# Layer 1's output projection: eight row tiles instead of five taken over six operand tiles inside the mixer

## The chip, the core and the metric

The kernel runs on one core of one Trainium2 chip. The metric is device time in microseconds (us) of one execution on that core, lower is better. The core's engines each run their own instruction stream in order and wait on one another by semaphores: PE is TensorE (matmuls; PEld is its weight load, which overlaps), DVE is VectorE, ACT is ScalarE, POOL is GpSimd, and SP issues most DMAs. In order listings, "x3" is three equal instructions in a row.

## The reference

A two-layer decoder trunk over 16 learned meta tokens and 1024 positions, width 1024. Layer 0 mixes by RWKV-7 and a pooling mixer, layer 1 by differential attention (8 heads). What the change touches is the end of layer 1's mixer:

```
h1 = rmsnorm(h, g0)
o  = differential_attention(h1)           # 8 heads of 128 -> 1024 values a position
y  = o @ w_out                            # "output projection": 1024 -> 1024
h  = h + rmsnorm(y, g1)
h  = h + rmsnorm(relu2(rmsnorm(h, g2) @ w1) @ w2, g3)   # MLP
```

Meta positions are dropped from the result. All is float32, with results close to float32's.

## The kernel before

Activations lie transposed: 128 features on the partitions, positions along the free dimension. A product in near-float32 is made of three matmuls in fp32r: each weight and each operand is split into a high part (a cast on ACT) and a low part (a subtraction on DVE, in the mixer on POOL), and high*high, low*high and high*low are accumulated. `wslices`/`mm3` write these in the mixer (L377, L378, L379), `mms` in what follows (L691).

**The output projection of layer 1** has 8 row tiles (128 output features each). Each sums over 8 operand tiles (one per attention head), for 4 quarters c0 to c3 of 256 positions. A full quarter of a row tile is 8 x 3 = 24 matmuls of 128x256. It is done in two stages:

- `early`, inside the mixer: for row tiles 0 to 4, the sum over operand tiles 0 to 5 (heads 0 to 5), 18 matmuls a quarter into the PSUM tile `pse`; ACT copies it to `pz` (L527) and stores it from its own DMA queue (L528) to `part`, a scratch tensor in DRAM. It is a generator that yields after each quarter. The list `fill` holds the operand loads of six heads, then the steps of `early`, with the load of operand tile 6 (`load(6)`) put nine places ahead of its end. During the last head, `fill[:30]` runs between the steps of attention, and the rest of it after. The weights of a row tile are loaded by SP (L360), cast by ACT (L361) and split by POOL (L362).
- `late`, after the mixer: for row tiles 0 to 4 the remaining operand tiles 6 and 7 (6 matmuls a quarter), which DVE adds (L721) onto `ac`, the tile into which `part` was loaded (L673). Row tiles 5 to 7 are taken over all 8 operand tiles here (24 matmuls a quarter), and ACT copies them to `ac` (L723). The weights of this stage are `LW[1]`: `wl` in two pieces (operand tiles 6 and 7 of row tiles 0 to 4, 640 columns each) and three pieces of `wo` (row tiles 5 to 7, 1024 columns). They are loaded by SP (L669), cast by ACT (L670) and split by DVE (L671).

`late` then works by halves of 512 positions (half 0 is c0 and c1, half 1 is c2 and c3). As the tiles of a half get complete, ACT squares them (L677, L682) and DVE sums the squares into `ss0` or `ss1` (L683). `scale` has PE sum `ss` over the partitions (L733); ACT and DVE make the inverse root (L741 to L743, L747, L748). `norms` scales the half and adds the residual on DVE (L768, L769, eight of each; the residual `hh` is loaded by L755), squares on ACT (L771) and sums by PE (L733). `base` makes the MLP's operands (ACT L809, DVE L810). `plain` is the first product of the MLP with two blocks of its first weights, loaded by L836 and split by L856 (ACT) and L857 (DVE); DVE L868 takes its result. After both halves the operands of a seven-product scheme are built (L885 to L895, L817 to L821), and the main loop of the MLP starts.

The order on each engine is not that of the text: `late` records its work in a `Flow` object, which orders it by estimated costs (`F.pe`, `F.act`, `F.dve`, `F.dma`); the mixer is ordered by a tile scheduler. SP issues its DMAs in order and waits at each for its buffer and its source.

Of the kernel before, what the change touches and what calls it, by code (L numbers as in the profile page):

```python
# [7 lines left out]
F32 = mybir.dt.float32  # L8
# [6 lines left out]
P = 128  # L15
T = 1040
# [44 lines left out]
PLAN = ((('prep', 0, 3), ('proj', (9, 5, 1), 1)), (('invert', 0, 1), ('prep', 1, 1), ('proj', (3, 6, 14, 2, 10), 1)), (('chain', 0, 1), ('invert', 1, 1), ('prep', 2, 1), ('proj', (15, 7, 11), 1), ('pool', (0, 1), 1)), (('invert', 2, 1), ('chain', 1, 1), ('prep', 3, 1), ('proj', (16, 17), 3), ('pool', (2, 3), 1), ('load', (0, 1), 2)), (('load', (2, 3, 4, 5), 18),), (('early', 8, 4), ('invert', 3, 3), ('chain', 2, 1)), (('early', 24, 1), ('chain', 3, 2)))  # L61


LW = ((768, 768, 1024, 1024), (640, 640, 1024, 1024, 1024))


AFTER = {"PE": (.25, 0.0), "ACT": (.17, .13), "DVE": (.11, .12), "POOL": (.08, .05), "SP": (.1, 0.0)}
# [254 lines left out]
class Trunk:  # L322
# [208 lines left out]
    def ahead(self, l):  # L531
# [4 lines left out]
        self.opb = [pool.tile([P, 4 * NH], F32R, name=self.nm("opb")) for _ in range((2, 3)[l])]  # L536
        n = self.lw_n = LW[l]
        at, self.lw_at = 0, []
# [15 lines left out]
    def late(self, l, xs, part, hin, hmid, hout, pre, rsb):  # L554

        nc, tc, A = self.nc, self.tc, self.A
# [2 lines left out]
        NS, SUB = ((2, 260), (1, 512))[l]  # L559
        NB = 8 // NS  # L560
        off = (0, NM)[l]
        ne = (6, 5)[l]
        chunks = QS[l]
        ends = (CH, QS[1])[l]
        stack = contextlib.ExitStack()
# [971 lines left out]
    def mixer0(self):  # L1537
# [10 lines left out]
        with tc.tile_pool(name="yp", bufs=4) as self.yp:  # L1548
# [41 lines left out]
            with tc.tile_pool(name="dps", bufs=2, space=PSUM, reuse_waits="tile") as self.dps, \  # L1590
# [31 lines left out]
                self.late_x = xs  # L1622
                self.lw_n = LW[0]
                for i in (0, 1):
# [12 lines left out]
    def mixer1(self, hn):  # L1637
        tc, nc, A, dr = self.tc, self.nc, self.A, self.dr
        self.o1d = dr.tile([8, P, 1024], F32, name="o1d")
        part = dr.tile([5 * P, T], F32, name="part1")  # L1640
        lam_init = 0.8 - 0.6 * math.exp(-0.3)
        with tc.tile_pool(name="dps", bufs=2, space=PSUM, reuse_waits="tile") as dps, \
             tc.tile_pool(name="sps", bufs=2, space=PSUM, reuse_waits="tile") as sps, \
             tc.tile_pool(name="tps", bufs=1, space=PSUM, reuse_waits="tile") as tps, \
             tc.tile_pool(name="aps", bufs=1, space=PSUM, reuse_waits="tile") as aps, \
             tc.tile_pool(name="ep", bufs=1, reuse_waits="tile") as ep:
            self.dps, self.sps, self.tps, self.aps, self.ep = dps, sps, tps, aps, ep
            self.tp = ep
            self.cs = ep.tile([P, 2, T], F32, name="cs")
            nc.sync.dma_start(self.cs, A["rope"])  # L1650
            lv = ep.tile([P, 4, C], F32, name="lv")
            nc.sync.dma_start(lv, A["lamv"])
            self.identb = ep.tile([P, P], mybir.dt.bfloat16, name="identb")
            nc.vector.tensor_copy(self.identb, self.con[:, K_ID:K_ID + P])
            self.maskb = ep.tile([P, P], mybir.dt.bfloat16, name="maskb")
            cau = ep.tile([P, 512], F32, tag="sb", name="cau", bufs=4)[:, :P]
            nc.sync.dma_start(cau, A["con"][:, K_CAU:K_CAU + P])
            nc.vector.tensor_copy(self.maskb, cau)
            nc.vector.tensor_tensor(lv[:, 0:2], lv[:, 0::2], lv[:, 1::2], op=ALU.mult)
            l2 = ep.tile([P, 2], F32, name="l2")  # L1660
            nc.vector.tensor_reduce(l2, lv[:, 0:2], axis=mybir.AxisListType.X, op=ALU.add)
            nc.scalar.activation(l2, l2, AF.Exp)
            self.nlam = ep.tile([P, 1], F32, name="nlam")
            nc.vector.scalar_tensor_tensor(self.nlam, l2[:, 1:2], -lam_init, l2[:, 0:1], op0=ALU.add, op1=ALU.subtract)
            self.sub = ep.tile([P, 1], F32, name="sub")
            nc.vector.tensor_scalar(self.sub, self.par[:, C_SUB:C_SUB + 1], (lam_init - 1.0) * 0.5 / P, None, op0=ALU.mult)
            self.pt, self.ov = {}, {}
            wide = [w.rearrange("p a b -> p (a b)") for w in self.WP]
            self.ring, self.turn = [(wide[0], wide[1]), (wide[2], ep.tile([P, 1024], F32R, name="wpx"))], 0
            self.given = [((wide[0], wide[1]),), (None,)]  # L1670
            self.quarters = QS[1]
            xs = [[] for _ in QS[1]]
            early = self.early(xs, A["wo_1"], part, 6, 5)
            load = lambda k: [0 for _ in self.loads(xs, self.o1d, (k,), NM, 2)]
            fill = [lambda k=k: load(k) for k in range(6)] + [lambda: next(early)] * (4 * 5)
            fill.insert(max(len(fill) - 9, 6), lambda: load(6))
            qkv, first = self.attn_in(0, hn)
            for i in [0, 5, 1, 6, 10, 11, 2, 7, 3, 4, 12, 8, 9, 13, 14, 15]:
                first[i]()
            for b in (0, 1):  # L1680
                self.pt[0, b] = self.attn_block(0, b, qkv)
            for h in range(8):
                nxt, side = self.attn_in(h + 1, hn) if h < 7 else (None, fill[:30])
                main = self.attn(h, qkv, nxt)
                at = (0, 6, 12, 12, 14, 15, 16, 24, 24, 24, 24, 24, 24, 24, 29, 29) if h < 7 else [0 + i * 2 for i in range(len(side))]
                i = 0
                for n, f in enumerate(main):
                    while i < len(side) and at[i] <= n:
                        side[i]()
                        i += 1  # L1690
                    f()
                for f in side[i:]:
                    f()
                qkv = nxt
            for f in fill[30:]:
                f()
            for c in range(4):
                xs[c].append(self.x7[c])
            self.late_x = xs
        return part  # L1700
# [384 lines left out]
```

## Time and profile before

| what | value |
|---|---|
| median of 3 runs | 2776.96 us (2776.26 to 2778.88) |
| the profiled execution's own time | 2771.01 us |
| its span in the trace | 2769.1 us |
| mean granted TensorE clock | 0.974 of full speed |
| PE busy | 94% of the span |
| DVE busy | 73% |
| ACT busy | 48% |

The profiled execution is 5.95 us shorter than the median of the runs; 1.9 us of its own time lie outside the span of the trace. Times in the rows below count from the start of the span. Layer 1's output projection lies at about 1939 to 2089 us, the norms and the first products of the MLP go on to about 2147 us, and the MLP's main loop follows to the end.

### The profile page before, as it was taken

Reading aid. Unit: us, or ns where it says so; the run is one execution under the profiler, and the core shown is the slowest. Engines: PE = TensorE matmul, PEld = TensorE weight load, DVE = VectorE, ACT = ScalarE, POOL = GpSimd, SP = SyncE. Lnnn points to the kernel's source line nnn. Section 1 sums busy time; section 2 is a strip of 40 time slices with the busy share of each in tenths; the row PEclk is TensorE's granted clock in tenths of the full one; section 3 lists DMA queues with packets and bytes.
Section 4 is the critical chain, followed back from the end, with each engine's and each line's share of the span. In section 5 each row is a group of like instructions: output and inputs, shape, how many; then the busy total and the mean of one; then the engine's idle time right before and its main releaser. Section 6 shows DMA issues by size and latency. Waiting matters only on the chain.

```text
span 2769.1 us, 44824 instructions
## 1 busy us (share of the span) xinstructions
PE 2614.2 (94%) x16950; PEld 2381.9 (86%) x16950; DVE 2032.5 (73%) x3742; ACT 1342.7 (48%) x2779; POOL 290.4 (10%) x410
## 2 busy tenths in 40 slices
PE   7999998899999999999968999999889999999997
PEld 6899897899899999999956899898787788778877
DVE  5356876534977777888786887888648778778888
ACT  5456776544633334343344556555636333443342
POOL 0111334220000000000012222222000000000000
PEclk9999998899999999999988999999999999999998
DMA  4456777554324345443332222222243243543443
GB/s 152 172 183 187 244 220 222 179 162 150 142 101 170 137 164 193 169 153 132 107 112 73 59 77 68 62 67 62 77 159 137 103 167 150 194 172 137 152 160 122
DMA packets 198575, 391.27 MB, mean 141 GB/s; under 512 B 59984, under 2 KB 122328, under 8 KB 185944
## 3 DMA queue, kind: packets, MB, share of 16 engines
q1 hardware_dynamic: 171176, 348.24, 37.8%
q10 hardware_dynamic: 27184, 40.18, 4.0%
q8 instruction: 133, 2.18, 0.3%
q14 instruction: 82, 0.67, 0.1%
HBM read 240.06 MB, written 131.38 MB: 134 GB/s over the span
## 4 chain that ended last, share of the span: by engine, by line
PE 64%; DVE 10%; ACT 4%; issue 2%; DMA 2%; POOL 0%; DVEq 0%; SPq 0%; ACTq 0%; POOLq 0%
PE bank L691 44%; PE psq L377 2%; PE psq L378 2%; PE psq L379 2%; PE ps L292 1%; PE s L1824 1%; PE tr L1870 1%; PE s L1826 1%; PE xs L292 1%; ACT p L1843 1%; DVE ac L1072 1%; DVE ac L1073 1%; DVE opb L818 1%; PE av L1896 1%; DVE ac L1001 1%
## 5 line engine op out<-in xcount | busy, mean ns | idle before, releaser
L691 PE MATMUL bank<-opa,wp 128*128 128x260 f32 (+1 forms) x3296 | 658.9, 320 | 8.6 <-DVE wp L782 5.3
L691 PEld LDWEIGHTS bank<-opa,wp 128*128 128x128 f32 x3296 | 518.0, 189 | 60.1 <-DVE wp L782 6.8
L691 PE MATMUL bank<-opb,wp 128*128 128x260 f32 (+1 forms) x1150 | 348.4, 324 | 1.8 <-DVE ac L1001 1.8
L292 PE MATMUL ps<-opa,whi 128*128 128x346 f32 (+2 forms) x1008 | 268.3, 328 | 4.7 <-DVE ys L292 4.0
L691 PE MATMUL bank<-opa,hh 128*128 128x260 f32 (+1 forms) x1112 | 241.1, 321 | 8.0 <-DVE hh L782 5.3
L691 PEld LDWEIGHTS bank<-opb,wp 128*128 128x128 f32 x1150 | 216.9, 189 | 21.0 <-ACT opa L1024 2.2
L1001 DVE TENSOR_TENSOR ac<-bank,ac 128x520 f32<-128x520 f32 (+1 forms) x256 | 171.6, 691 | 67.8 <-PE bank L691 66.5
L691 PE MATMUL bank<-opa,opb 128*128 128x260 f32 (+4 forms) x1168 | 206.1, 306 | 11.6 <-ACT opb L670 7.2
L691 PEld LDWEIGHTS bank<-opa,hh 128*128 128x128 f32 x1112 | 185.9, 191 | 24.4 <-DVE hh L782 5.8
L691 PEld LDWEIGHTS bank<-opa,opb 128*128 128x128 f32 x1168 | 168.2, 194 | 22.6 <-ACT opb L670 7.6
L292 PEld LDWEIGHTS ps<-opa,whi 128*128 128x128 f32 x1008 | 181.1, 192 | 6.5 <-DVE ys L292 4.8
L691 PE MATMUL bank<-opb,hh 128*128 128x260 f32 (+1 forms) x616 | 180.6, 327 | 0.0
L781 ACT CAST wp<-raw 128x512 fp32r<-128x512 f32 (+1 forms) x138 | 80.3, 584 | 184.6 <-PE bank L691 179.0
L292 PE MATMUL ps<-opa,wlo 128*128 128x346 f32 (+2 forms) x504 | 158.4, 314 | 0.0
L781 ACT CAST wp<-ss 128x512 fp32r<-128x512 f32 (+1 forms) x130 | 76.7, 590 | 164.5 <-PE bank L691 143.6
L1843 ACT ACTIVATE p<-s,m 128x272 f32<-128x272 f32 (+7 forms) x128 | 95.4, 750 | 85.4 <-DVE m L1839 83.6
L691 PE MATMUL bank<-opa,tt 128*128 128x260 f32 (+1 forms) x648 | 130.5, 318 | 0.2 <-DVE tt L782 0.2
L691 PEld LDWEIGHTS bank<-opb,hh 128*128 128x128 f32 x616 | 117.7, 191 | 9.9
L377 PE MATMUL psq<-opa,wp 128*128 128x346 f32 (+2 forms) x352 | 117.5, 334 | 4.4 <-DVE rp L462 2.6
L362 POOL TENSOR_TENSOR wpx<-raw,wp 128x1024 fp32r<-128x1024 f32 (+1 forms) x14 | 34.4, 2459 | 785.8 <-PE bank L691 742.8
L379 PE MATMUL psq<-opa,wp 128*128 128x346 f32 (+2 forms) x352 | 113.4, 322 | 0.0
L691 PE MATMUL bank<-opb,opb 128*128 128x256 f32 (+4 forms) x456 | 111.3, 308 | 0.5 <-DVE tt L747 0.5
(408 smaller groups left out, 6561.9 us busy)
## 6 DMA issues: line engine op xcount, KB each, us to landing
raw<-in_w_dram SPq DMA_DIRECT2D x64, 1024.0 KB
hid<-ac SPq DMA_DIRECT2D x14, 1820.0 KB
hid<-ac SPq DMA_DIRECT2D x14, 1792.0 KB
hh<-hid SPq DMA_DIRECT2D x23, 1040.0 KB
hh<-hid SPq DMA_DIRECT2D x23, 1024.0 KB
pk<-sg ACTq DMA_DIRECT2D x32, 704.0 KB
lt<-pk SPq DMA_DIRECT2D x32, 704.0 KB
raw<-in_w_qkv_dram SPq DMA_DIRECT2D x24, 512.0 KB
```

What stands on the lines that cost most here:

```text
L292: one = eng, cost, lambda: fn(*args, **kw), r, w
L362: (lo or nc.gpsimd).tensor_tensor(lw[:, :n], raw[:, :n], hi[:, :n].bitcast(F32), op=ALU.subtract)
L377: nc.tensor.matmul(ps, wh, xh, start=(first and i == 0), stop=False)
L378: nc.tensor.matmul(ps, wl, xh, start=False, stop=False)
L379: nc.tensor.matmul(ps, wh, xl, start=False, stop=(last and i == n - 1))
L691: nc.tensor.matmul(ps, use(x), use(y), start=start and i == j == 0, stop=i == len(ws) - 1 and j == 2, skip_group_check=not start)
L781: F.act(n, lambda: nc.scalar.copy(use(t[0][:, :n]), src), r=rd, w=[z[0]] + claim)
L818: F.dve(4 * NH, lambda: tt(lo, use(src), hi.bitcast(F32), op=ALU.subtract), r=rd + wh, w=wl)
L1001: F.dve(NH, lambda d=d, q=q: tt(sv(d), q, sv(d), op=ALU.add), r=nq + nd, w=nd, ps=True)
L1072: F.dve(W, lambda d=d, k=k: stt(d, d, self.gcol(l, 3, k), y, op0=ALU.mult, op1=ALU.mult), r=nd + [ny], w=nd)
L1073: F.dve(W, lambda d=d, k=k: tt(d, d, use(H3[k // 4][:, k % 4, :W]), op=ALU.add), r=nd + [("H", k // 4, k % 4)], w=nd)
L1843: nc.scalar.activation(p[:, :L0], S[c][:, :L0], AF.Exp, bias=m2[:, c:c + 1], scale=0.125, accum_out=m2[:, 2 + c:3 + c])
```

## The change

`ne`, the number of row tiles that are taken over six operand tiles inside the mixer, goes from 5 to 8. So `early` does all eight row tiles and `part` has eight; `late` has 6 matmuls per quarter of every row tile, all added by DVE onto what `part` holds. The late weights are then two pieces of 1024 columns, and no `wo` pieces. `fill` has twelve entries more, and `load(6)` stands at its place 29 instead of 17.

```
-LW = ((768, 768, 1024, 1024), (640, 640, 1024, 1024, 1024))
+LW = ((768, 768, 1024, 1024), (1024, 1024))
...
-        ne = (6, 5)[l]
+        ne = (6, 8)[l]
...
-        part = dr.tile([5 * P, T], F32, name="part1")
+        part = dr.tile([8 * P, T], F32, name="part1")
...
-            early = self.early(xs, A["wo_1"], part, 6, 5)
+            early = self.early(xs, A["wo_1"], part, 6, 8)
             load = lambda k: [0 for _ in self.loads(xs, self.o1d, (k,), NM, 2)]
-            fill = [lambda k=k: load(k) for k in range(6)] + [lambda: next(early)] * (4 * 5)
+            fill = [lambda k=k: load(k) for k in range(6)] + [lambda: next(early)] * (4 * 8)
             fill.insert(max(len(fill) - 9, 6), lambda: load(6))
```

What it does to SP's order where `late` begins, first before, then after. `raw` are the two staging buffers of weights (`raw0` the one that the mixer uses too), `ac0` and `ac1` the two halves, `h2` the residual, `w1` the MLP's first weights.

```order
L360 DMA raw0_743<-in_wo_1_dram 128x768
L669 DMA raw0_743<-in_wl_1_dram 128x640
L669 DMA raw_20234<-in_wo_1_dram 128x1024 x2
L673 DMA ac0_20243<-part1_13700 128x5x512
L669 DMA raw0_743<-in_wl_1_dram 128x640
L755 DMA hh2355_20241<-h2_68 128x4x512
L755 DMA hh2356_20242<-h2_68 128x4x512
L673 DMA ac1_20244<-part1_13700 128x5x512
L669 DMA raw0_743<-in_wo_1_dram 128x1024
L836 DMA raw_20234<-in_w1_1_dram 128x2048
```

```order
L360 DMA raw0_743<-in_wo_1_dram 128x768 x4
L673 DMA ac0_20516<-part1_13700 128x8x512
L669 DMA raw0_743<-in_wl_1_dram 128x1024 x2
L755 DMA hh2379_20514<-h2_68 128x4x512
L755 DMA hh2380_20515<-h2_68 128x4x512
L673 DMA ac1_20517<-part1_13700 128x8x512
L836 DMA raw_20507<-in_w1_1_dram 128x2048
L836 DMA raw0_743<-in_w1_1_dram 128x2048
```

Before, one `wl` piece and two `wo` pieces stand ahead of the first load from `part`; after, no late weights do, and both `wl` pieces stand behind it.

PE's order from the last matmul of `early`, first before, then after (the first rows of each; `bank` is a PSUM tile, `opa` an operand of the projection, `opb` a split weight):

```order
L379 MATMUL pse2344_20191<-opa7_77,wp1252_6332 128x256
L691 MATMUL bank5_20250<-opa0_70,opb2347_20223 128x256
L691 MATMUL bank5_20250<-opa0_70,opb2348_20224 128x256
L691 MATMUL bank5_20250<-opa0_70,opb2347_20223 128x256 x2
L691 MATMUL bank5_20250<-opa0_70,opb2348_20224 128x256
```

```order
L379 MATMUL pse2368_20464<-opa7_77,wp1254_6334 128x256
L691 MATMUL bank0_20518<-opa1_71,opb2370_20495 128x256 x3
L691 MATMUL bank0_20518<-opa1_71,opb2371_20496 128x256 x3
L691 MATMUL bank1_20519<-opa1_71,opb2370_20495 128x256 x3
L691 MATMUL bank1_20519<-opa1_71,opb2371_20496 128x256 x3
```

Before, `late` opens with a full tile over eight operand tiles from the `wo` weights; after, with tiles of six matmuls, each of which needs both `wl` pieces. After `early` PE has 216 matmuls less: the row sum of `ss0` stood behind 204 matmuls of half 0 and 48 of half 1, and stands behind 96 and 30 now.

DVE's order around the scaling of half 0, first before, then after (`ac1` is half 1, `opb` in L857 a weight of the MLP):

```order
L683 TENSOR_TENSOR ss0_20236<-ss0_20236,tt2352_20238 128x512
L747 SCALAR_TENSOR_TENSOR tt2353_20239<-bank0_20245,tt2353_20239 128x512
L748 SCALAR_TENSOR_TENSOR tt2354_20240<-tt2353_20239,tt2354_20240 128x512
L768 SCALAR_TENSOR_TENSOR ac0_20243<-ac0_20243,par_61,tt2354_20240 128x512 x2
L769 TENSOR_TENSOR ac0_20243<-ac0_20243,hh2355_20241 128x512 x2
```

```order
L857 TENSOR_TENSOR opb2373_20504<-raw_20507,opb2373_20504 128x512
L857 TENSOR_TENSOR opa7_77<-raw0_743,opa7_77 128x512
L721 TENSOR_TENSOR ac1_20517<-ac1_20517,bank3_20521 128x256
L857 TENSOR_TENSOR opb2372_20497<-raw0_743,opb2372_20497 128x512
L721 TENSOR_TENSOR ac1_20517<-ac1_20517,bank6_20524 128x256
L747 SCALAR_TENSOR_TENSOR tt2377_20512<-bank0_20518,tt2377_20512 128x512
L748 SCALAR_TENSOR_TENSOR tt2378_20513<-tt2377_20512,tt2378_20513 128x512
L721 TENSOR_TENSOR ac1_20517<-ac1_20517,bank4_20522 128x256
L768 SCALAR_TENSOR_TENSOR ac0_20516<-ac0_20516,par_61,tt2378_20513 128x512 x2
```

Eight of half 1's sixteen adds (L721) and three of the eight L857 now stand ahead of the first L768; before, all ten of half 1's adds and all eight L857 stood behind the eight L768 and L769. From L810 on, and in the MLP's main loop, the order of DVE, ACT, PE and SP is the same as before but for single places.

## Rows read from the trace of the kernel before

**Rows 1.** The page of the profile: the span, and busy time of each engine with its share and instructions.

```profile
span 2769.1 us, 44824 instructions
...
PE 2614.2 (94%) x16950; PEld 2381.9 (86%) x16950; DVE 2032.5 (73%) x3742; ACT 1342.7 (48%) x2779; POOL 290.4 (10%) x410
```

**Rows 2.** Busy time of the engines in stretches of the span, whole program. Columns: stretch, its length in us, then for each engine busy us (and instructions), the granted TensorE clock as a share of full speed, the DMA engines' busy share, and what they moved.

```profile
1950.00:1970.00 20.00, 14.12 (x72) 10.85 (x72) 15.72 (x33) 13.35 (x31) 0.19 (x1) 0.84 0.23 73
2015.60:2024.10 8.50, 8.50 (x74) 8.43 (x72) 0.70 (x2) 1.68 (x5) 0.00 (x0) 1.00 0.40 108
2024.10:2031.40 7.30, 0.70 (x3) 0.28 (x1) 2.07 (x3) 3.19 (x4) 0.00 (x0) 0.75 1.00 378
2031.40:2035.20 3.80, 3.77 (x20) 3.77 (x21) 1.11 (x1) 0.00 (x0) 0.00 (x0) 0.59 1.05 388
2035.20:2039.00 3.80, 3.80 (x35) 3.80 (x34) 0.83 (x1) 1.32 (x3) 0.00 (x0) 1.00 1.05 397
2031.40:2062.50 31.10, 31.07 (x252) 31.07 (x252) 12.03 (x20) 9.05 (x17) 0.00 (x0) 0.95 0.43 165
2105.00:2147.00 42.00, 37.54 (x146) 26.98 (x144) 40.35 (x53) 26.11 (x35) 0.00 (x0) 1.00 0.25 93
```

**Rows 3.** PE in order of time where `early` ends and `late` begins. Columns: start, us, engine, line, operation, out<-in, shape, count, and in brackets the idle time before with what ended it.

```profile
2023.95 0.27 PE L379 MATMUL pse<-opa,wp 128*128 128x256 f32 x1
2028.80 0.58 PE L691 MATMUL bank<-opa,opb 128*128 128x256 f32 x1 [4.57 <-ACT opb L670]
2031.43 31.23 PE L691 MATMUL bank<-opa,opb 128*128 128x256 f32 x251 [2.06 <-DVE opb L671]
2062.50 1.02 PE L733 MATMUL bank<-ss,con 128*128 128x512 f32 x2
```

**Rows 4.** The instructions of the tiles `pse` and `pz`: count, then duration in ns (least, median, most), first and last start.

```profile
L377 PE MATMUL pse<-opa,wp x120: 274/281/681, 1939.5 to 2023.7; 128*128 128x256 f32 x120
...
L527 ACT COPY pz<-pse x20: 353/373/385, 1971.7 to 2024.3; 128x256 f32<-128x256 f32 x20
```

**Rows 5.** Weights of `early` on POOL: the same columns.

```profile
L362 POOL TENSOR_TENSOR wp<-raw,wp x13: 1834/2392/2815, 1446.1 to 2004.8; 128x1024 fp32r<-128x1024 f32 x10, 128x768 fp32r<-128x768 f32 x3
```

**Rows 6.** SP's DMA queue in order of time: start and length of an issue.

```profile
2022.22 0.38 SPq L673 DMA_DIRECT2D ac<-part  x1
2022.65 0.52 SPq L669 DMA_DIRECT2D raw<-in_wl_dram  x1
2023.21 1.70 SPq L755 DMA_DIRECT2D hh<-h  x2
2030.04 0.36 SPq L673 DMA_DIRECT2D ac<-part  x1
2030.44 0.53 SPq L669 DMA_DIRECT2D raw<-in_wo_dram  x1
2032.54 17.59 SPq L836 DMA_DIRECT2D raw<-in_w_dram  x2
```

**Rows 7.** What SP's queue waited for between 2020 and 2045 us: in total, times, longest.

```profile
SPq L836 <- DMA raw<-in_wo_dram: 7.0, 1, 7.0
```

**Rows 8.** ACT and its DMA queue, then DVE, in order of time, at the stores of `early` and the weights of `late`.

```profile
2020.41 0.33 ACTq L528 DMA_DIRECT2D part<-pz  x1
...
2030.00 1.04 ACT L670 CAST opb<-raw 128x1024 fp32r<-128x1024 f32 x1 [1.26 <-DMA part<-pz]
...
2030.15 2.36 DVE L671 TENSOR_TENSOR opb<-raw,opb 128x1024 fp32r<-128x1024 f32 x2 [3.54 <-DMA part<-pz]
```

**Rows 9.** DVE in order of time at the scaling of half 0.

```profile
2065.61 0.69 DVE L747 SCALAR_TENSOR_TENSOR tt<-bank,tt 128x512 f32<-128x512 f32 x1 [3.99 <-ACT tt L743]
...
2067.06 1.42 DVE L768 SCALAR_TENSOR_TENSOR ac<-ac,par,tt 128x512 f32<-128x512 f32 x2
...
2075.98 1.29 DVE L769 TENSOR_TENSOR ac<-ac,hh 128x512 f32<-128x512 f32 x2
```

**Rows 10.** DVE's groups between 2024 and 2147 us: count, busy us, mean ns of one, idle before.

```profile
L683 DVE TENSOR_TENSOR ss<-ss,tt 128x512 f32<-128x512 f32 x14 | 9.7, 691 | 5.5 <-ACT tt L682 4.8
L721 DVE TENSOR_TENSOR ac<-ac,bank 128x256 f32<-128x256 f32 x20 | 8.1, 420 | 9.7 <-PE bank L691 9.7
L857 DVE TENSOR_TENSOR opb<-raw,opb 128x512 fp32r<-128x512 f32 x6 | 3.9, 687 | 0.0
```

**Rows 11.** DVE in order of time: its waits between the scaling of half 0 and the main loop, and the main loop's first instruction.

```profile
2088.80 0.42 DVE L721 TENSOR_TENSOR ac<-ac,bank 128x256 f32<-128x256 f32 x1 [1.05 <-PE bank L691]
...
2101.47 0.69 DVE L868 SCALAR_TENSOR_TENSOR ss<-bank,rsb 128x512 f32<-128x512 f32 x1 [2.27 <-PE bank L733]
...
2103.52 0.69 DVE L747 SCALAR_TENSOR_TENSOR tt<-bank,tt 128x512 f32<-128x512 f32 x1 [1.36 <-ACT tt L743]
...
2140.53 0.69 DVE L868 SCALAR_TENSOR_TENSOR ss<-bank,rsb 128x512 f32<-128x512 f32 x1 [0.95 <-PE bank L691]
...
2146.62 0.68 DVE L782 TENSOR_TENSOR hh<-raw,hh 128x512 fp32r<-128x512 f32 x1
```

**Rows 12.** PE in order of time: the first product of the MLP, and the main loop's wait.

```profile
2089.07 0.39 PE L691 MATMUL bank<-opb,opb 128*128 128x512 f32 x1
...
2147.35 0.79 PE L691 MATMUL bank<-opa,hh 128*128 128x512 f32 x1 [2.26 <-DVE hh L782]
```

## The prediction

> **What bounds the kernel now.** The page comes first: PE is busy 94% of the span, DVE 73% [rows 1]. So on the whole matmuls set the time, and a change that keeps their number, as this one does, can only give or take where PE waits. The change reaches from the end of the mixer to the start of the MLP's main loop, so that stretch is read next, by the busy time of its parts [rows 2]. PE is full while `early` runs, nearly idle from 2024.1 to 2031.4 us, full until 2062.5, and at the end, from 2105 to 2147, it is DVE that is full (40.35 us of 42.0) while PE has 4.5 us to spare. The orders of time say why. `late` opens with a gap of 7.4 us between the end of `early` (2023.95 + 0.12 = 2024.07) and 2031.43, but for one matmul of 24 at 2028.80 [rows 3]: it waits for weights, and in that gap the DMA engines are busy all the time [rows 2]. After that stretch the first scaling on DVE starts at 2067.06 [rows 9], and the MLP's main loop starts when DVE has made its operands: PE waits 2.26 us for DVE at 2147.35 [rows 12]. From 2067.06 to 2146.62, when DVE turns to the main loop, its waits of 0.9 us or more are the four of [rows 11], 5.6 us together. So once half 0 is summed, **DVE's chain bounds the stretch**, and the question is when that chain begins.
>
> **The change, part by part.**
>
> *Matmuls.* 216 of 128x256 (3 row tiles, 4 quarters, 18) leave `late` and join `early`. In `early` 72 take 8.50 us [rows 2], 0.118 each; in `late` 251 take 31.07 [rows 2, 3], 0.124 each with the cold start in it, and 35 in 3.80 (0.109) right after it. The same work at the same price: no gain by itself. `early` now ends at 2024.07 + 216 x 0.118 (25.5) = E = 2049.6.
>
> *Copies and weights of `early`.* ACT gets 12 copies of 0.37 us [rows 4] and loses 12 of the same length in `late`; both lie beside PE. The three more weights take about 1.84 us each on POOL (the least of [rows 5], the narrow shape), against 8.5 us of matmuls per row tile, and are made one row tile ahead: hidden. Without that cover each would cost its 1.84 on PE.
>
> *Late weights.* Before, a `wl` and two `wo` pieces were issued ahead of the load from `part`; PE could begin with row tiles 5 and 6. After, each late tile needs both `wl` pieces, and both stand behind the load of half 0 of `part` on SP. That load can be issued only when c1 of the last row tile is stored: at 2022.22, 1.85 us ahead of the end of `early` [rows 6], its store having been issued at 2020.41 [rows 8]. So the new issue time is E - 1.85. It carries 2.10 MB (1024 rows by 512 by 4 bytes), was 1.31; each `wl` piece is 0.52 MB. The late weights of before, the `wo` piece issued at 2030.44, landed at about 2039.9: of the two DMAs behind it the second waited 7.0 us for it, from 2032.9 on [rows 6, 7]. From 2022.22 to 2039.9 that queue moved 1.31 + 0.33 + 2.10 + 1.31 + 0.52 = 5.57 MB in 17.7 us. At 397 GB/s [rows 2] these are 14.0 us, and 3.7 more for latency and what is left of other transfers. By the same price the second `wl` piece lands (2.10 + 1.05) / 0.397 + 3.7 = 11.6 us after the issue, at E + 9.8. Then ACT casts it (1.04, [rows 8]) and DVE subtracts (2.36 for two, 1.18, same rows): PE is at full work at E + 12.1 with 0.1 for the handoff, in place of E + 7.4. **The gap grows by about 4.7 us**, to 2061.7. Bounds: 7.4 if the weights came as fast as before, some 14 if the rate in the gap is the 378 GB/s of its row and stores of `early` still hold the queue.
>
> On that gap the Trainium skill speaks, in "DMA: Bandwidth & Descriptors", section "Queues, rings and completion order": all DMAs that SP issues share one queue row, and on each DMA engine the descriptors of a ring are consumed in order. By it nothing overtakes the load from `part`, and the gap is the 12.1 us; were the two served side by side, the weights would be there when 2.1 MB have moved, and the gap 9.4. The 7.0 us wait for the `wo` piece [rows 7] agrees with the first.
>
> *Cold start.* After the gap of before the granted clock was 0.59 for 3.8 us, with 20 matmuls where the next 3.8 us had 35 [rows 2], a loss of 15 x 0.109 = 1.6 us. After a longer gap the same loss stands once more.
>
> *Up to half 0's row sum.* Before it stood behind 252 matmuls, at 2062.50 [rows 3]. Now it stands behind 96 of half 0 and 30 of half 1: 126 x 0.118 = 14.9, with 1.6 for the cold start 16.5: 2061.7 + 16.5 = 2078.2. DVE has in that time 16 adds of half 0 (0.42 each), 7 sums (0.69) [rows 10] and some 6 us of half 1's adds and MLP weights, 17.5 us at most: close to PE's, and so not counted but kept as a risk. The **scaling of half 0 starts 15.7 us later**, plus an add of 0.42 that stands ahead of L768: +16.1, at 2083.2.
>
> *From there.* DVE has 2.9 us less behind that point: three L857 (0.69) and two adds (0.42) were drawn ahead of it [rows 10]. Of its 5.6 us of waits [rows 11] the two of PE's plain work (1.05 and 0.95) go, since PE then has more time ahead; those of 2.27 and 1.36 follow half 1's row sum through ACT and stay, as that sum comes last on PE again. 16.1 - 2.9 - 2.0 = **+11.2 us** at the main loop, whose order is the old one and which adds nothing. Bounds: all 5.6 absorbed gives +7.6, nothing but the 2.0 waits gives +14.1.
>
> *The MLP's first weights* (L836, 2 x 1.05 MB) are now queued behind `part` half 0, `wl`, `hh` and `part` half 1: 9.44 MB after the issue, 23.8 + 3.7 us, at E + 25.6. On ACT six casts of them, on DVE three L857 stand ahead of half 0's root, which is due at E + 29. They are hidden by some 2 us.
>
> Sum, against the profiled execution's 2771.01: 2782.2. It lies 5.95 under the median, so for the median **2776.96 + 11.2 = 2788.2, said as 2788.0**.
>
> **The rivals.**
>
> *PE stays the bound.* If DVE's chain had more slack than its rows say, only the longer gap is paid: +4.7 us, 2781.7, within 0.2% (5.6 us, about what a measurement of this kernel tells from no change). For it: PE is busy 94% of the span. Against: from 2105 on DVE is 96% busy [rows 2] and PE waits for it. It decides if the first product of the MLP (2089.07 before, [rows 12]) doesn't wait at each of DVE's L810.
>
> *Nothing is absorbed.* The 16.1 us come through whole: 2793.1, and about 2 more if the MLP's weights land over 2 us late or the clock falls once more as PE waits through the scaling. For it: the row sums of half 0's norm now stand on PE with few tiles between them, so PE waits there, and may go cold as it did in the first gap (0.59, [rows 2]). Against: 2.9 us of DVE's work has demonstrably moved ahead in its order.
>
> *Faster: the added row tiles fill PE's idle time in the last head.* From 1950 to 1970 PE is busy for 14.12 us of 20 [rows 2]. If 10 us of the added matmuls ran there and in the like stretch before, E would fall by 10, and with PE as the bound the end by 10 - 4.7: 2771.7. It decides from 4.7 us of filled idle time with DVE not in the way, 16.1 with it. Against: in PE's order the added matmuls stand behind those of row tile 4, and the last head's stretch is the same as before.
>
> **How the numbers follow.** The forecast (+7.6 to +14.1) 0.65; nothing absorbed, with the clock or the late weights, 0.16; PE stays the bound 0.15; faster 0.04. The range holds the first two and half of the third: 2780.5 to 2795.0. The forecast's cases and "nothing absorbed" are slower by over 0.2%: 0.81; the same 0.15; faster 0.04.
>
> **What would show it.** The profile of after: the first L691 of `late` some 12 us after the last L379, with DMA at full share; the L733 of `ss0` near 2078 and the first L768 near 2083; the MLP's first product near 2097 with waits on L810; L782 on DVE at about 2158; the main loop as long as before. The prediction is wrong if `wl` lands ahead of `part`, if the first L768 comes before 2079, or if DVE shows waits over 8 us between it and L782.

## The result, and the profile after

| | before | after |
|---|---|---|
| median | 2776.61 us (6 runs) | 2786.92 us (6 runs) |
| profiled span | 2769.1 us | 2784.9 us |
| ratio of times | | 1.0036, 95% interval 1.0025 to 1.0048 |

The change makes the kernel 10 us slower (7 to 13 by the interval); 2788.0 was forecast, with a range of 2780.5 to 2795.0. The two profiled executions differ by more, 15.8 us, but not all of that belongs to the change: `early` starts at 1939.5 in the one and 1942.9 in the other, on the same code before it, and from the main loop's first L782 to the end it is 622.5 and 624.9 us, on the same code too. So the executions are compared by two stretches inside them: the length of `early`, and **D**, from the end of `early` to L782. PE where `early` ends, in order of time, after (the rows that answer to [rows 3]):

```profile
2052.94 0.28 PE L379 MATMUL pse<-opa,wp 128*128 128x256 f32 x1
2062.56 0.58 PE L691 MATMUL bank<-opa,opb 128*128 128x256 f32 x1 [9.34 <-ACT opb L670]
2063.82 1.01 PE L691 MATMUL bank<-opa,opb 128*128 128x256 f32 x3 [0.68 <-DVE opb L671]
2065.11 16.01 PE L691 MATMUL bank<-opa,opb 128*128 128x256 f32 x122 [0.28 <-DVE opb L671]
2080.97 1.02 PE L733 MATMUL bank<-ss,con 128*128 128x512 f32 x2
```

`early` ends at 2053.06: 110.1 us after its start, 84.6 before, so 25.6 longer. The gap to full work is 12.05 us, 7.36 before. The row sum of `ss0` comes 27.9 us after the end of `early`, 38.4 before. Then SP's DMA queue and ACT in the gap, after (as [rows 6, 8]):

```profile
2051.24 0.38 SPq L673 DMA_DIRECT2D ac<-part  x1
2051.71 1.87 SPq L669 DMA_DIRECT2D raw<-in_wl_dram  x2
...
2061.46 1.04 ACT L670 CAST opb<-raw 128x1024 fp32r<-128x1024 f32 x1 [7.83 <-DMA raw<-in_wl_dram]
2062.75 1.05 ACT L670 CAST opb<-raw 128x1024 fp32r<-128x1024 f32 x1 [0.24 <-DMA raw<-in_wl_dram]
```

Both casts are released by the landing of `wl`, which was issued right behind the load from `part`. The granted clock is low behind the gap as it was before ([rows 2]): 21 matmuls in the first stretch, 34 in the next.

```profile
2065.10:2068.90 3.80, 3.79 (x21) 3.79 (x22) 1.26 (x3) 0.00 (x0) 0.00 (x0) 0.63 1.05 386
2068.90:2072.70 3.80, 3.80 (x34) 3.80 (x34) 2.78 (x7) 1.32 (x3) 0.00 (x0) 1.00 1.07 396
```

And DVE, after (as [rows 9, 11]):

```profile
2085.74 1.41 DVE L768 SCALAR_TENSOR_TENSOR ac<-ac,par,tt 128x512 f32<-128x512 f32 x2
...
2115.89 0.69 DVE L868 SCALAR_TENSOR_TENSOR ss<-bank,rsb 128x512 f32<-128x512 f32 x1 [1.61 <-PE bank L733]
...
2117.94 0.69 DVE L747 SCALAR_TENSOR_TENSOR tt<-bank,tt 128x512 f32<-128x512 f32 x1 [1.36 <-ACT tt L743]
...
2160.01 0.69 DVE L782 TENSOR_TENSOR hh<-raw,hh 128x512 fp32r<-128x512 f32 x1
```

Half 0's scaling starts 32.7 us after the end of `early` (43.0 before); counted from the start of `early`, it is 15.3 us later. The two waits of about 1 us on PE's plain work ([rows 11]) are gone, the other two are there. D is 106.95 us, 122.55 before. 25.6 - 15.6 = **+10.0 us** at the main loop: this is the measured loss, and it lies in this stretch. The ratios below leave out two executions, of 3229.66 us (four row tiles) and 8873.02 us (three), that lie far above all others of their kernels.

### The profile page after: what moved, and what is told of

It is laid out like the page before. It is cut to its first block, busy times and chain, and to the rows that moved or that the text cites. A ratio compares the mean times of both kernels' runs of the same rounds, so it can differ in the third digit from the quotient of the medians.

```text
span 2784.9 us, 44875 instructions
## 1 busy us (share of the span) xinstructions
PE 2617.6 (94%) x16950; PEld 2381.0 (85%) x16950; DVE 2038.3 (73%) x3751; ACT 1342.6 (48%) x2779; POOL 296.6 (11%) x413
## 4 chain that ended last, share of the span: by engine, by line
PE 63%; DVE 10%; ACT 4%; issue 2%; DMA 2%; SPq 0%; POOL 0%; DVEq 0%; ACTq 0%; POOLq 0%
PE bank L691 43%; PE psq L377 2%; PE psq L378 2%; PE psq L379 2%; PE ps L292 1%; PE s L1824 1%; PE tr L1870 1%; PE s L1826 1%; PE xs L292 1%; ACT p L1843 1%; DVE ac L1072 1%; DMA hh<-hid 1%; PE pse L377 1%; PE pse L378 1%; DVE opb L818 1%
## 5 line engine op out<-in xcount | busy, mean ns | idle before, releaser
L691 PE MATMUL bank<-opa,opb 128*128 128x260 f32 (+4 forms) x952 | 179.6, 311 | 15.2 <-ACT opb L670 11.9
L691 PEld LDWEIGHTS bank<-opa,opb 128*128 128x128 f32 x952 | 142.5, 195 | 25.5 <-ACT opb L670 12.3
```

The source lines that it names most:

```text
L691: nc.tensor.matmul(ps, use(x), use(y), start=start and i == j == 0, stop=i == len(ws) - 1 and j == 2, skip_group_check=not start)
```

## The experiments

All runs are set beside the kernel before on the same chip. "Local" is (length of `early` - 84.6) + (D - 122.55), from the profile of each; where `early` is longer or shorter than its matmuls make it by a fall of the clock within the last head, the text says so. The last column is the ratio in us of the kernel before.

| row tiles | what (`pz` below) | gap | D | local | measured ratio (95%) | in us |
|---|---|---|---|---|---|---|
| 8 | the changed kernel | 12.05 | 106.95 | +10.0 | 1.0036 (1.0025 to 1.0048) | +10 |
| 8 | `wl` ahead of `part` | 6.2 | 103.99 | +10.3 | 1.0024 (1.0011 to 1.0036) | +7 |
| 8 | `hh` ahead of `wl` | 19.35 | 114.24 | +17.3 | 1.0051 (1.0037 to 1.0064) | +14 |
| 8 | `wl` ahead, own `pz` | 4.7 | 105.30 | +8.3 | 1.0023 (1.0010 to 1.0035) | +6 |
| 5 | before, own `pz` | 3.95 | 120.19 | -2.3 | 0.9986 (0.9972 to 1.0000) | -4 |
| 7 | | 9.95 | 111.94 | +9.8 | 1.0015 (1.0003 to 1.0027) | +4 |
| 6 | first | 8.6 | 122.99 | +12.3 | 1.0042 (1.0030 to 1.0054) | +12 |
| 6 | second | 8.4 | 122.97 | +9.4 | 1.0033 (1.0018 to 1.0048) | +9 |
| 6 | own `pz` | 3.3, later 0.6 | 117.01 | +3.1 | 1.0013 (1.0002 to 1.0023) | +4 |
| 4 | | 2.4 | 123.88 | -7.1 | 0.9977 (0.9964 to 0.9991) | -6 |
| 4 | own `pz` | 2.4 | 123.49 | -7.5 | 0.9972 (0.9958 to 0.9985) | -8 |
| 3 | own `pz` | 11.2 | 145.65 | +2.8 | 1.0004 (0.9993 to 1.0015) | +1 |

**The queue.** First, the `wl` pieces ahead of the load from `part`, with the order on PE, ACT and DVE untouched:

```
-  F.dma(lambda raw=raw, i=i: nc.sync.dma_start(raw, self.lw_src(l, i)), ...)
+  F.dma(lambda raw=raw, i=i: None if l and i < 2 else nc.sync.dma_start(raw, self.lw_src(l, i)), ...)
-  F.dma(lambda h=i: nc.sync.dma_start(m[h][:, :ne], self.rows(part, off + NH * h, NH)), ...)
+  F.dma(lambda h=i: part_load(h), ...)   # for l and h == 0: both wl loads, then this one
```

> The changed kernel with one thing different: SP issues both wl pieces ahead of the load of half 0 from part; the order on PE, ACT and DVE is that of the changed kernel. D is the time from the end of early (the last L379) to the main loop's first L782 on DVE: 122.5 us before, 107.0 after, where early ends 25.5 us later; so after stands at +9.9. Theory (the gap is made by the queue, and half 0's scaling starts DVE's chain, which nothing absorbs any more): the gap falls from 12.1 to about 6.0, since the cast of the second wl piece then waits for a store of early whose buffer it takes over, and D falls by the same 6 to 101; time about +4 over before, 2781. Rival A (DVE's chain is bound elsewhere, by the load of part or of the MLP's weights): the gap falls and D stays at 105 to 107, time +8 to +10. Rival B (the loss is the added copies, stores and bytes): gap and D stay, time +10.

The gap fell to 6.2 as expected, and half 0's scaling came 4.4 us sooner after the end of `early`; D fell by 3.0, not 6. The clock took back the rest, in two places: more of its low stretch lay behind the shorter gap, and it fell once more behind half 1's scaling. These are its stretches right behind the gap, then that one (columns as in [rows 2]):

```profile
2071.00:2075.00 4.00, 4.00 (x19) 4.00 (x20) 1.26 (x3) 0.00 (x0) 0.00 (x0) 0.50 1.05 392
2075.00:2079.00 4.00, 4.00 (x28) 4.00 (x28) 1.82 (x5) 1.27 (x2) 0.00 (x0) 0.74 1.05 387
...
2140.00:2145.00 5.00, 5.00 (x18) 3.62 (x18) 5.00 (x9) 4.12 (x5) 0.00 (x0) 0.81 0.12 43
```

19 and 28 matmuls in two stretches of 4 us; in the changed kernel one stretch of 3.8 us was slow, and the next had 34. The low stretch itself is as long as in the changed kernel, 10 us; it began sooner, and the gap ended sooner still (the rows are in the last section). And behind half 1's scaling, where the changed kernel shows 1.00, the clock was 0.81, and DVE waited 1.4 us more there. (In this execution `early` took 3.3 us more than in the changed kernel's, on the same order, at a clock of 0.5 within the last head; without that the local sum is +7.0.) So the place in SP's queue is worth some 3 of the 10 us by D; the two ratios' intervals overlap. Rival B falls, since gap and D both moved; between the theory's D of 101 and rival A's 105 to 107 the run does not decide.

The opposite dose, `hh` between `part` and `wl`:

```
-  F.dma(lambda raw=raw, i=i: nc.sync.dma_start(raw, self.lw_src(l, i)), ...)
+  F.dma(lambda raw=raw, i=i: wl_load(raw, i), ...)   # for l and i == 0: both hh loads, then this one
-  F.dma(lambda q=q: nc.sync.dma_start(H[q], ...), ...)
+  F.dma(lambda q=q: None if l and not h else nc.sync.dma_start(H[q], ...), ...)
```

> The changed kernel with the two loads of the residual hh (2.1 MB) issued between the load of half 0 from part and the wl pieces, so that these are 2.1 MB further back; all else in the same order. Theory: 2.1 MB at 0.397 MB a us are 5.3 us: gap 12.1 to 17.4, D 107.0 to 112.3, time about +15 over before. Rival A (slack of some us behind the gap): gap 17.4, D 108 to 110. Rival C (transfers of one queue are served side by side): the gap grows by under 3 us.

The gap grew to 19.35 and D to 114.24, 7.3 more in both: **behind the gap nothing absorbs any of it**. Rivals A and C fall. The size was off: 2.1 MB took 7.3 us and not 5.3. SP needed 4.3 us to issue the two `hh` loads, but that is not where the time went: the DMA engines were full all the while. These are the issues, a stretch of the gap (columns as in [rows 2]), the second cast, and what SP's queue moved from the issue of the load from `part` to that cast (packets, MB, share of the 16 engines), last the same for the changed kernel:

```profile
2049.95 4.30 SPq L678 DMA_DIRECT2D hh<-h  x2
2054.34 3.28 SPq L679 DMA_DIRECT2D raw<-in_wl_dram  x2
...
2053.00:2068.00 15.00, 0.00 (x0) 0.00 (x0) 0.00 (x0) 0.96 (x1) 0.00 (x0) 0.61 1.04 396
...
2068.34 1.04 ACT L670 CAST opb<-raw 128x1024 fp32r<-128x1024 f32 x1 [0.25 <-DMA raw<-in_wl_dram]
...
q1 hardware_dynamic: 2933, 6.37, 92.5%
...
q1 hardware_dynamic: 1520, 3.54, 84.7%
```

The loads up to the second `wl` piece are 5.24 MB here and 3.15 MB in the changed kernel. So 1.1 MB of loads that were issued behind it had moved by then, where it was 0.4 MB: 2.8 MB more at 0.396 MB a us are 7.1 us.

**The memory of `pz`.** In [rows 8] the casts and splits of the `wo` pieces, which SP had issued ahead of the load from `part`, are released by a store of `pz`: these late weights lie where `pz` lay. One line at the start of the mixer's pool gives `pz` a place of its own:

```
             self.cs = ep.tile([P, 2, T], F32, name="cs")
+            pz = [self.tmp("pz", 2) for _ in (0, 1)]
```

> The kernel before with the two pz buffers at a place of their own, all orders unchanged. In the kernel before the casts L670 at 2027.70 and the split L671 at 2030.15 are released by stores of pz. Theory (the gap of 7.4 us there was the stores of early, not the weights, which had been loaded): the casts follow one another after the last copy, gap 7.4 to about 4.5, D 122.5 to 119.5, time about 3 us under before. Rival (the gap was the weights' transfer): gap 7.4 and time unchanged.

The casts now follow the last copy of `early` at once (all three without a wait), and the gap is 3.95:

```profile
2033.21 0.37 ACT L527 COPY pz<-pse 128x256 f32<-128x256 f32 x1 [1.74 <-PE pse L379]
2033.62 0.33 ACTq L528 DMA_DIRECT2D part<-pz  x1
2033.98 2.62 ACT L670 CAST opb<-raw 128x640 fp32r<-128x640 f32 x3 [0.40 <-ACT pz L527]
```

So in the kernel before 3.4 of the gap's 7.4 us were a wait for stores; the rest is the last copy and the first casts and splits, not the weights' transfer. D fell by 2.4, less than the gap's 3.4: more of the low clock lies behind this gap (last section). The ratio's interval reaches 1, so the time alone would not show it. The same line on top of the first experiment:

> As the first, and the two pz buffers of early get a place of their own at the start of the mixer's pool, so that no late weight takes over their memory. Theory: the casts follow the last copy of early on ACT: 0.6 + 2 x 1.04, then DVE's split of the second piece 1.2 behind: gap 4.0, D 99, time +2 over before. If the memory of pz is not what the cast waits for, it stays as in the first run, gap 6, D 101.

That missed. The gap fell to 4.7, but the scaling of half 0 came no sooner (28.2 us after the end of `early`, 28.3 without the line): DVE's first adds wait for the load of `part`, and its last sum waits for a square on ACT. That square stands behind a cast of the MLP's weights (L862 here), which waits for their load; then PE waits for DVE. With a fall of the clock behind half 1's scaling D was 1.3 longer.

```profile
2057.73 1.08 DVE L727 TENSOR_TENSOR ac<-ac,bank 128x256 f32<-128x256 f32 x3 [2.65 <-DMA ac<-part]
...
2071.25 0.62 ACT L862 CAST opb<-raw 128x512 fp32r<-128x512 f32 x1 [2.70 <-DMA raw<-in_w_dram]
...
2072.43 0.69 DVE L689 TENSOR_TENSOR ss<-ss,tt 128x512 f32<-128x512 f32 x1 [2.74 <-ACT tt L688]
...
2073.18 1.12 PE L739 MATMUL bank<-ss,con 128*128 128x512 f32 x2 [1.75 <-DVE ss L689]
```

So with eight row tiles weights that come still sooner gain nothing in this order: the load of `part`, which lands 7.3 us after `early`, and that of the MLP's weights hold the chain instead. What the kernel would take without the second wait was not tried.

**The number of row tiles.** Each takes the places of the diff with another number, as here for four:

```
-LW = (..., (1024, 1024))
+LW = (..., (512, 512, 1024, 1024, 1024, 1024))
-        ne = (6, 8)[l]
+        ne = (6, 4)[l]
...                                   # part, early and fill in the same way
```

Seven (two pieces of 896, one of 1024):

> Seven row tiles in early (wl of 896 columns, one wo piece); SP now issues the wo piece and both wl pieces behind the load of half 0 from part, as in the changed kernel. Theory: early ends 17.0 us later, the gap is 10 (1.84 + 0.52 MB at 0.397 MB a us and 3.7, 1.9 ahead of the end, then cast and split) in place of 7.4, the row sum stands behind 174 matmuls (9.2 us less): half 0's scaling 10.4 later; DVE has four L857 and two adds less behind it (3.6), and up to 2.0 of PE's waits go: +5 to +7. Rival linear: +6.6. Rival only the gap: +2.6.

D was 111.94: with the 17.0 us that two row tiles add to `early`, +6.4, as the theory gives. (`early` was 3.4 us longer than that by the clock, as in the first experiment.) The ratio says +4, 1 to 7. Six (two pieces of 768, two of 1024):

> Six row tiles in early (wl of 768 columns, two wo pieces), nothing else. The first row tiles of late have their wo pieces ahead of part, as before. Theory (half 0's row sum stands behind fewer matmuls, and the gap only grows where wl comes after part): early ends 8.5 us later, the gap stays 7.4, the row sum stands behind 216 matmuls in place of 252 (4.2 us less), so half 0's scaling starts 4.2 us later; DVE has two L857 and one add less behind it (1.8 us): +2 over before. Rival (the loss is linear in the row tiles, as copies, stores and bytes are): +3.3. Rival (only the gap counts): 0.

This missed by 10 us; 3.3 of them are `early` at a low clock. The view of ACT's waits between 2038 and 2050 names another part, and the order of time shows where:

```profile
ACT opb L670 <- DMA part<-pz: 5.7, 1, 5.7
...
2045.27 1.99 ACT L670 CAST opb<-raw 128x1024 fp32r<-128x1024 f32 x2 [5.66 <-DMA part<-pz]
```

Here the cast of the first `wo` piece waits for the store of the *last* `pz`, which lands 5.6 us after its issue; so the gap was 8.6 where 7.4 was expected, and more of the low clock lay behind it. It was run again, and once with `pz` at a place of its own:

> Six row tiles in early, a second time: the first time it stood at +11 over before where +2 was expected. By its trace the gap was 8.6 (+1.2), the granted clock was 0.5 for 8 us inside the last head (early lasted 96.4 us, 3.3 more than 8.5 us a row tile give), and it fell again behind half 1's scaling, where DVE waited 2.5 us for PE's row sum. If these falls of the clock are this order's own, it stands at +9 to +12 again; if they came by chance in that hour, at +2 to +5.

> Six row tiles, and pz at a place of its own, so that the casts of the wo pieces don't wait for the stores of early (5.66 us of wait in the first run with six). Theory: gap 8.6 to about 3.5, and 4 to 5 us less time than the same kernel without it. Rival (the second wait there is the weights' transfer): gap and time as without it.

Again +9, with D the same to 0.02 us, and `early` at its regular length: the fall of the clock in the last head came by chance, the rest is that order's own. With `pz` apart, D is 6.0 less and the time +4, near the +2 that was expected at first: the store was worth 6 us with six row tiles. The gap became as short as expected: PE was at work 3.3 us after `early`, and waited only 0.55 us more later, since the cast of the second `wo` piece still waited for a store of `pz`:

```profile
2036.49 4.36 PE L691 MATMUL bank<-opa,opb 128*128 128x256 f32 x24 [0.88 <-DVE opb L671]
2039.03 1.05 ACT L670 CAST opb<-raw 128x1024 fp32r<-128x1024 f32 x1 [3.85 <-DMA part<-pz]
2041.39 22.81 PE L691 MATMUL bank<-opa,opb 128*128 128x256 f32 x191 [0.55 <-DVE opb L671]
```

The new place of `pz` seems to be that of another late tile; that was not followed further. What stays in all three runs with six is a longer way from half 0's scaling to L782: 82.5, 81.6 and 81.4 us, where the expectation makes 77.8 (79.6 less 1.8). DVE waits there for PE before an add of half 1, as here in the second run; the expectation had left that wait out:

```profile
2104.40 0.42 DVE L721 TENSOR_TENSOR ac<-ac,bank 128x256 f32<-128x256 f32 x1 [3.09 <-PE bank L691]
```

The other direction, four:

> The other direction: four row tiles in early (wl of 512 columns, four wo pieces); SP issues both wl and two wo pieces ahead of part, and PE begins late with tiles of six matmuls. Theory: early ends 8.5 us sooner, the row sum stands behind 288 matmuls in place of 252 (4.2 more), the gap is between 5 (casts of 512 columns are short, but wait for a store of early) and 7.4: half 0's scaling 4 to 6 us sooner and the main loop 3 to 6 sooner, if the later wo pieces are in time: 2771 to 2774. Rival (PE stays the bound, all else being hidden): 0 to -2.

> As the one with four row tiles, and pz at a place of its own. Theory: the casts (0.6 each) and the split follow the last copy, gap 3.0, so 4 us less than in the kernel before; with the 4 us that the earlier scaling gives, 7 to 8 under before: 2769 to 2770. Rival (the clock falls again after the short gap and takes back 2 to 3 us, or a later wo piece is late): 4 to 5 under before.

Both are faster than before, **0.9977 and 0.9972**; the place of `pz` makes no difference that these runs can tell, since the `wl` casts don't wait for it in either. So the gap is 2.4 without it too, where 5 to 7.4 was expected. With four, SP issues both `wl` pieces and two `wo` pieces ahead of the load from `part`, PE waits 1.5 us, and the clock does not fall at the gap (four row tiles, `pz` apart; the gap, the stretch right behind it, and the last stretch up to the main loop):

```profile
2023.00:2025.40 2.40, 0.58 (x4) 0.22 (x2) 1.50 (x4) 2.00 (x5) 0.00 (x0) 1.00 1.04 393
2025.40:2029.20 3.80, 3.80 (x30) 3.62 (x31) 3.62 (x6) 1.61 (x2) 0.00 (x0) 1.00 1.06 401
2101.20:2146.50 45.30, 42.40 (x168) 31.20 (x166) 40.60 (x55) 27.24 (x37) 0.00 (x0) 1.00 0.28 104
```

In the last stretch PE is now the fuller engine, 42.4 of 45.3 us, where DVE was (40.35 of 42.0, [rows 2]), and DVE waits for it:

```profile
2131.99 2.29 DVE L818 TENSOR_TENSOR opb<-hh,opa 128x2048 fp32r<-128x2048 f32 x1 [3.33 <-PE bank L691]
```

So going down from five the bound seemed to pass to PE, and three should give nothing more:

> Three row tiles in early, pz at a place of its own. With four, DVE's chain waits 3.3 us for PE before the main loop, so PE bounds the stretch there. Theory: no more than 1 us sooner than with four, 6 to 9 under before, or later by some us if the fifth wo piece is late (SP issues three of the five behind the load of half 1 of part). Rival (each row tile that leaves early gives 3 to 4 us): 10 to 12 under before.

It gives back nearly all: +1. With three, `early` ends before the last head's attention does, and no matmuls of it are left to run beside the norm of that head (L1918 to L1931 here). ACT casts the first late weights only after that norm, and PE waits 6.04 us. (Gap and D of this row hold the end of the attention too, so they don't compare with the other rows; the local sum does.)

```profile
2013.18 1.12 PE L1918 MATMUL pn<-sb,con 128*128 128x512 f32 x2 [0.69 <-ACT sb L1910]
...
2019.25 2.82 ACT L670 CAST opb<-raw 128x1024 fp32r<-128x1024 f32 x4
2020.34 0.58 PE L691 MATMUL bank<-opa,opb 128*128 128x256 f32 x1 [6.04 <-ACT opb L670]
```

So neither the theory (no more than 1 us from four) nor the rival came. Whether three with a better order would equal four was not tried.

## Why the prediction was right, step by step

- **`early` 25.5 us longer**: 25.6. The added matmuls cost what they cost in `late`, and their weights and copies were hidden.
- **The gap 12.1 in place of 7.4**: 12.05 and 7.36. The second `wl` piece was put at 9.8 us after the end of `early`; its cast starts at 9.7, released by the landing. The page of the Trainium skill that was cited, "DMA: Bandwidth & Descriptors" ("Queues, rings and completion order"), agrees: served side by side it would have been 9.4. That nothing overtakes is too strong, though: 0.4 MB of later loads had moved by then, and 1.1 MB in the run with `hh` ahead. There the same price, 0.397 MB a us, missed by 2.0 us, so that the gap came out within 0.1 us is in part luck.
- **What the gap of before was**: the reading that PE waits there for weights was half right: it waits for their casts and splits, but the weights had landed, and 3.4 us of the wait were for stores. [rows 8] had the answer, `<-DMA part<-pz`, and the run with `pz` apart shows it: gap 3.95. It didn't change the sum, which took 7.4 as measured.
- **Cold start 1.6 us, once**: 21 matmuls in 3.8 us, then 34, so 13 x 0.11 = 1.4. That this loss comes once more after a longer gap was no law: behind shorter gaps it was larger (last section).
- **Half 0's scaling +16.1**: 15.3. The row sum came 27.9 us after `early`, where 28.6 was worked out.
- **4.9 us absorbed behind it**: 5.3 (from L768 to L782 79.6 before, 74.3 after). The waits that were to go are gone, the waits that were to stay stayed, one of them 0.7 shorter.
- **The MLP's weights hidden**: their first cast starts without a wait, and the main loop's order and its start behind DVE are as before.
- **The rivals.** PE as the bound (+4.7) falls by the loss itself, +10.0 at the main loop and 7 at least by the interval, and by the last 42 us up to the main loop, in which DVE is full after the change too (first of the rows below). The sign that was named, waits of the MLP's first product on L810, did not appear: PE waited ahead of that product, in the norm's row sums, for ACT (second row), and the product began at 2099.36 without a wait (third). That 7.3 us of gap came through as 7.3 in the run with `hh` ahead fits PE as the bound as well, so it does not decide. That nothing is absorbed (+16) didn't come: 5.3 us were. Filled idle time in the last head did not come either: `early` took the full 25.6.

```profile
2118.00:2160.00 42.00, 36.71 (x140) 25.66 (x138) 41.22 (x54) 26.55 (x36) 0.00 (x0) 1.00 0.25 93
...
2088.47 2.26 PE L733 MATMUL bank<-tt,con 128*128 128x512 f32 x4 [1.51 <-ACT tt L771]
...
2099.36 0.63 PE L691 MATMUL bank<-opa,opa 128*128 128x512 f32 x2
```

Of the 10 us some 3 are the weights' place behind `part` (the first experiment). The other 7 are the rest of the sum: `early` grew by 8.5 us a row tile, the row sum of half 0 has 126 matmuls fewer ahead of it (some 15 us), and 5.3 us are absorbed. No run isolates this part; the runs with seven and four row tiles fit it, those with six and three lost time elsewhere.

## What to carry to other kernels

Work moved ahead of a point where another engine's chain begins delays that chain, even when the number of matmuls stays the same: what counts is how much stands *before* the first result that the chain needs. Here 25.6 us more ahead, 126 matmuls fewer behind (some 15) and 4.7 us more of gap made 15.3. A load whose source is written late should not stand ahead of weights on an in-order DMA queue. And where an idle time is released by a *store* of a tile that the waiting instruction has nothing to do with, look at whose memory the new tile takes over: a place of its own for `pz` was worth 2.4 us of D with five row tiles, 6.0 with six, and nothing that the runs can tell with four. With four row tiles and `pz` apart the kernel is 0.28% faster than the one it started from (0.15% to 0.42%).

## What the runs showed of the hardware

A store of 128 KB from ACT's queue landed within 1.8 us of its issue while no load was moving (2020.41 to the issue of L673 at 2022.22, which waited for it, [rows 6, 8]), and 5.4 us after it when SP's loads were in flight (2024.66 to 2030.04, the next L673). These are ACT's row of the second store, and the two stretches (columns as in [rows 2]); in the first the store is all that moves:

```profile
2024.66 0.33 ACTq L528 DMA_DIRECT2D part<-pz  x1
...
2020.40:2022.20 1.80, 1.80 (x18) 1.80 (x17) 0.00 (x0) 0.05 (x1) 0.00 (x0) 1.00 0.22 73
2024.66:2030.04 5.38, 0.58 (x1) 0.28 (x1) 0.82 (x1) 1.81 (x3) 0.00 (x0) 0.78 1.04 401
```

So loads on another queue held up a small store threefold.

What a gap in PE's work costs by the granted clock isn't in step with the gap's length: its low level (0.50, the lower of two) begins inside the gap, and only what is left of it when PE is at work again costs time. These rows show the stretch from the end of `early` to the fall, then the low one, in four kernels: before, changed, `wl` ahead of `part`, five row tiles with `pz` apart.

```profile
2024.07:2027.60 3.53, 0.15 (x2) 0.00 (x0) 0.82 (x1) 1.10 (x2) 0.00 (x0) 1.00 0.95 347
2027.70:2034.40 6.70, 3.55 (x15) 3.25 (x16) 2.36 (x2) 2.09 (x2) 0.00 (x0) 0.50 1.05 397
...
2053.06:2057.60 4.54, 0.16 (x2) 0.00 (x0) 0.00 (x0) 0.37 (x1) 0.00 (x0) 1.00 0.96 365
2057.80:2067.80 10.00, 4.28 (x16) 3.69 (x17) 3.29 (x4) 2.09 (x2) 0.00 (x0) 0.50 1.04 397
...
2064.73:2066.70 1.97, 0.16 (x2) 0.00 (x0) 0.00 (x0) 1.10 (x2) 0.00 (x0) 1.00 0.91 329
2066.90:2077.00 10.10, 8.06 (x32) 7.18 (x33) 4.29 (x7) 1.17 (x2) 0.00 (x0) 0.50 1.05 395
...
2033.02:2035.60 2.58, 0.16 (x2) 0.00 (x0) 0.83 (x1) 1.99 (x4) 0.00 (x0) 1.00 0.91 338
2035.80:2042.50 6.70, 6.02 (x27) 5.73 (x28) 2.34 (x2) 1.02 (x2) 0.00 (x0) 0.50 1.05 400
```

The gaps were 7.4, 12.05, 6.2 and 3.95 us; of the low stretches 3.0, 2.7, 6.1 and 5.5 us lay behind them. After 2.4 us, of which PE was idle for 1.8, the clock stayed at 1.00 (the rows with four row tiles).
